# Feed-forward gates and ups with the weights as standing operand, and weight remainders shared with GpSimd

## The chip, the cores and the metric

One core of one Trainium2 chip runs the whole program. The metric is the device time of one execution in microseconds (us), as a median of three runs. Changes of under 0.2% (3.9 us) are not told from none.

## What is computed

The input is 256 tokens of 1024 features. Four layers follow one another (two of a first block, two of a second), and each is feed-forward, mixer, feed-forward:

```python
def swiglu(x, w_gu, w_down):
    g, u = jnp.split(x @ w_gu, 2, axis=-1)
    return (jax.nn.silu(g) * u) @ w_down
...
for l in range(DEPTH):
    f = swiglu(rms_norm(x, ffn1_pre_g[l]), ffn1_w_gu[l], ffn1_w_down[l])
    x = x + 0.5 * rms_norm(f, ffn1_post_g[l])
    m = hybrid_mixer(rms_norm(x, mix_pre_g[l]), ...)
    x = x + rms_norm(m, mix_post_g[l])
    f = swiglu(rms_norm(x, ffn2_pre_g[l]), ffn2_w_gu[l], ffn2_w_down[l])
    x = x + 0.5 * rms_norm(f, ffn2_post_g[l])
```

The second block does the same with other mixers and without the norms behind. The gate and the up matrix are 1024 x 2816 each, the down matrix 2816 x 1024. All is float32. The kernel multiplies in float32r, a rounded form, and so splits each operand in a high part (the rounded value) and a low part (the remainder), and adds three products: high by high, high by low, low by high.

## The kernel before

The tokens lie in two tiles of 128 (t = 0 and 1), and each is a thread of its own (`thread`, a Python generator). Weights come from one packed stream in units of at most 128 x 1024 numbers. For each unit SyncE loads `raw`, then ScalarE or VectorE rounds it to `whi` (`split_hi`), then VectorE subtracts to get the low part `wlo` (`split_lo`). There are 6, 9 and 9 buffers of these; a `whi` and a `wlo` are given back when both threads have used the unit. Hence one thread leads the other by nine units at most.

In a feed-forward block (`ffn`) the tile of activations, transposed, is the standing operand of TensorE and the weights are streamed: for every 128 input features and every 512 columns of gate or up, `mm3` issues three products of 512 columns into `acc`, with `xTh` (high), `xTh` and `xTl` (low) standing:

```python
return [T.matmul(out_, kh, wh, start=start, stop=False), T.matmul(out_, kh, wl, start=False, stop=False),
        T.matmul(out_, kl, wh, start=False, stop=stop)]
```

The result has tokens as rows. ScalarE takes the silu of the gate with the row's norm factor `rs` as a scale (`act`), VectorE multiplies by the up (`fin`), and `t_hilo` transposes the product in pieces of 128 x 128 on TensorE (`tmp<-ident,scr`), since `down` needs the features as rows; its high and low part go to `big0` or `big1`. `down` then runs 22 units with the hidden tile standing, at 12 products of 512 columns a unit for both tiles. Behind it `postnorm` (in the first block) forms the sum of squares on ScalarE, the power -0.5 on GpSimd (`rsyo`), and updates `x` on VectorE; `prenorm` transposes the new `x` and forms `rs`, with another power on GpSimd (`rs`).

The order on each engine is fixed before the run: `Sched` plays the threads through with a cost per instruction (`Engine.make`), takes the most urgent of what can start (a priority from the longest chain behind it, plus a number of the table `BIAS`), and issues in that order; `Either` leaves the choice of engine to it. Where it foresees that TensorE will stand idle, `filler` puts in products with `warm` that compute nothing.

Of the kernel before, what the change touches and what calls it, by code (L numbers as in the profile page):

```python
# [21 lines left out]
P = 128  # L22
# [27 lines left out]
NHI = 9  # L50
NLO = 9
BIAS = {
    ("act", 3): -10.5, ("fin", 3): -1.5, ("fin", 4): -0.5, ("gains", 3): 22.0, ("gains", 4): -12.0,
    ("gate", 3): -7.0, ("gate", 4): -10.5, ("go", 4): -35.5, ("latents", 4): 7.5, ("lru", 4): 3.5, ("norm", 3): 0.5,
    ("norm", 4): 16.4, ("ret_g", 4): -4.5, ("ret_qk", 3): -0.5, ("ret_v", 3): -7.3, ("ret_v", 4): 6.8,
    ("retention", 3): 10.7, ("retention", 4): 1.0, ("sgu", 4): -2.2, ("t_hilo", 4): -5.8, ("thread", 4): -1.6,
    ("xbc", 4): 19.1,
}
IN_ORDER = ("xbc", "xbc2", "zdt", "lru", "sgu", "gate")
OUT_ORDER = (6, 7, 0, 1, 2, 3, 4, 5)  # L60
# [9 lines left out]
X_AFTER = {-1: (0, 0), 0: (1, 0), 2: (0, 1), 4: (1, 1)}  # L70
SCR = 6
LATER = 24
TMP = 4


def _plan():
    units = []

    def proj(specs):
        for cols in specs:  # L80
            n = 2 if units else 1
            for k in range(0, KT, n):
                units.append((list(range(k, k + n)), cols, None))

    def ffn(gate, up, down, l, up0):
        for c0 in range(0, FF, 512):
            if c0 + 512 <= FF:
                proj([[(gate, l, c0, c0 + 512)], [(up, l, up0 + c0, up0 + c0 + 512)]])
            else:
                proj([[(gate, l, c0, FF), (up, l, up0 + c0, up0 + FF)]])  # L90
# [228 lines left out]
class Engine:  # L319
# [233 lines left out]
def program(S, nc, pool, psp, x, wst, pfm, prow, post, lnp, mats, ret_dec, inv, pos, out):  # L553
# [10 lines left out]
    def acc_done(t):  # L564
        S.release(acc_pool[t])
# [38 lines left out]
    def scr_done():  # L604
        S.release(scr_pool)
# [25 lines left out]
    mhalf = pool.tile([P, 3], F32, name="mhalf")  # L631
    nc.vector.memset(mhalf, -0.5)
    early = pool.tile([P, 1], F32, name="early")
# [60 lines left out]
    def split_lo():  # L694
        for i, u in enumerate(units):
# [111 lines left out]
    def t_hilo(src, n, hi, lo, gain=None, evs=None, after=None):  # L807

        for b in range(0, n, 4):
# [20 lines left out]
            if evs is not None and gain is None:  # L830
                S.fire(evs[b // 4])

    def act_t(t):
        h = pool.tile([P, KT, P], F32R, tag=f"xTh{t}", name=f"xTh{t}", align_bytes=256)
        l = pool.tile([P, KT, P], F32R, tag=f"xTl{t}", name=f"xTl{t}", align_bytes=256)
        return h, l

    def prenorm(t, gain, late=False):

# [62 lines left out]
            q.dma_start(pgs[i], post[i:i + 1, :].to_broadcast([P, D]))  # L902
        return pgs[i]

    def ffn(t, gain, pgi, kpi=None):
        kh, kl, evs, rs, rs_ev = prenorm(t, gain, pgi == 0)
        hT = pool.tile([P, 2, FT, P], F32R, tag=f"big{t}", name=f"big{t}", align_bytes=256)
        hh, hl = hT[:, 0], hT[:, 1]
        hev = [Event() for _ in range(6)]

        def act(g, s, n, ev):
            yield rs_ev
            yield A.activation(s[:, :n], g[:, :n], AF.Silu, scale=rs)
# [12 lines left out]
        for c in range(6):
            n = 512 if c < 5 else 256
            g = yield from proj(t, kh, kl, evs)
            s = yield from scr()
            ev = Event()  # L930
            S.spawn(act(g, s, n, ev))
            if c < 5:
                u = yield from proj(t, kh, kl, evs)
            else:
                u = g[:, n:]
            S.spawn(fin(c, s, u[:, :n], n, ev))
            if c == 3 and t == 0:
# [4 lines left out]
        accs = yield from down(t, hh, hl, FT, lambda k: hev[k // 4])  # L942
        if pgi is not None:
            postnorm(t, accs, pgs[pgi], True)
        else:
            addback(t, accs, True)
# [760 lines left out]
    def thread(t):  # L1707
        yield
        for l in range(2):
            yield from ffn(t, fmc("ffn1_pre_g", l) if l else fm0, 3 * l, l)  # L1710
            yield from mixer1(t, l)
            yield from ffn(t, fmc("ffn2_pre_g", l), 3 * l + 2)
        for l in range(2):
            yield from ffn(t, fmc("ffn1_norm_2", l), None)
            yield from mixer2(t, l)
            yield from ffn(t, fmc("ffn2_norm_2", l), None)
        for j in range(2):
            yield xev[t][j]
            sl = slice(j * 512, (j + 1) * 512)
# [82 lines left out]
```

## Time and profile before

| what | value |
|---|---|
| median of 3 runs | 1938.17 us (1938.04 to 1938.38) |
| the profiled execution, time | 1938.33 us |
| the profiled execution, span from first to last instruction | 1936.6 us |
| TensorE matmuls, busy | 1925.4 us, 9247 instructions |
| VectorE, busy | 1494.3 us (77%), 2385 instructions |
| ScalarE, busy | 626.9 us (32%), 1136 instructions |
| GpSimd, busy | 52.9 us (3%), 76 instructions |
| read from HBM | 344 MB, 178 GB/s over the span |

The span leaves out 1.7 us of the execution's time. TensorE's records overlap: one of 512 columns lasts 0.39 us while the next begins 0.23 us after it, so what a product costs is read from start to start. The same holds for VectorE and ScalarE, whose records overlap by some 0.08 and 0.1 us.

### The profile page before, as it was taken

How to read it: one execution, taken by the hardware profiler on the slowest of the kernel's cores; microseconds unless marked ns; L12 is line 12 of the kernel's file. 1: busy time of each engine (PE TensorE's matmuls, PEld its weight loads, DVE VectorE, ACT ScalarE, POOL GpSimd, SP SyncE). 2: the span in 40 equal slices, each digit the busy share in tenths (PEclk: the TensorE clock that was granted, in tenths of full speed). 3: DMA queues.
4: the chain of work that ended last, by engine and by line, in shares of the span. 5: the costliest groups of instructions: out<-in, count | busy, mean ns of one | idle time of the engine just before them, and what ended most of it. 6: DMA issues, size and time to landing. Idle time of an engine off the chain costs nothing.

```text
span 1936.6 us, 24594 instructions
## 1 busy us (share of the span) xinstructions
PE 1925.4 (99%) x9247; PEld 1612.1 (83%) x9247; DVE 1494.3 (77%) x2385; ACT 626.9 (32%) x1136; POOL 52.9 (3%) x76
## 2 busy tenths in 40 slices
PE   9999999999999999999999999999999999999999
PEld 7888988888888898888888888888888888888887
DVE  7977898767767799776777779877777777987774
ACT  5211774211321287320232036631022102662220
POOL 1000010000000001000000000000000000000000
PEclk9999999999999999999999999999999999999999
DMA  8555546555655554654655554356565655545572
GB/s 317 179 191 177 166 148 196 195 167 194 224 177 182 180 168 145 199 190 163 208 186 183 185 180 155 125 178 184 180 203 174 184 181 184 159 126 170 178 217 65
DMA packets 98390, 346.89 MB, mean 179 GB/s; under 512 B 11424, under 2 KB 11680, under 8 KB 98272
## 3 DMA queue, kind: packets, MB, share of 16 engines
q1 hardware_dynamic: 97040, 341.26, 54.3%
q0 software_dynamic: 1088, 4.06, 0.6%
q8 instruction: 72, 1.18, 0.3%
q14 instruction: 46, 0.38, 0.1%
q10 hardware_dynamic: 144, 0.00, 0.0%
HBM read 344.24 MB, written 1.05 MB: 178 GB/s over the span
## 4 chain that ended last, share of the span: by engine, by line
PE 96%; ACT 2%; DVE 1%; POOL 0%; issue 0%; POOLq 0%
PE acc L469 89%; PE tmp L469 7%; ACT big L469 1%; ACT L469 1%; POOL rsyo L469 0%; PE tmp L595 0%; DVE wlo L469 0%; DVE x L469 0%; ACT whi L469 0%; DVE whi L469 0%; DVE big L469 0%; DVE scr L469 0%; ACT scr L469 0%; ACT xTh L469 0%; DVE rswo L469 0%
## 5 line engine op out<-in xcount | busy, mean ns | idle before, releaser
L469 DVE TENSOR_TENSOR wlo<-raw,whi 128x1024 fp32r<-128x1024 f32 (+4 forms) x638 | 765.3, 1201 | 56.1 <-ACT whi L469 43.1
L469 PE MATMUL acc<-whi,xTh 128*128 128x512 f32 (+3 forms) x1888 | 745.1, 395 | 0.0
L469 PE MATMUL acc<-wlo,xTh 128*128 128x512 f32 (+3 forms) x1888 | 729.5, 386 | 1.0 <-DVE wlo L469 1.0
L469 PE MATMUL acc<-whi,xTl 128*128 128x512 f32 (+3 forms) x1888 | 730.0, 387 | 0.0
L469 DVE CAST whi<-raw 128x1024 fp32r<-128x1024 f32 (+1 forms) x402 | 278.4, 692 | 260.7 <-PE acc L469 250.7
L469 PE MATMUL acc<-whi,big 128*128 128x512 f32 x1408 | 457.8, 392 | 0.0
L469 PEld LDWEIGHTS acc<-whi,xTl 128*128 128x128 f32 x1888 | 354.6, 188 | 69.7
L469 PEld LDWEIGHTS acc<-wlo,xTh 128*128 128x128 f32 x1888 | 355.4, 188 | 66.1 <-DVE wlo L469 3.7
L469 PEld LDWEIGHTS acc<-whi,xTh 128*128 128x128 f32 x1888 | 355.0, 188 | 63.8 <-ACT big L469 0.4
L469 ACT CAST whi<-raw 128x1024 fp32r<-128x1024 f32 (+4 forms) x236 | 235.1, 1004 | 303.3 <-PE acc L469 283.7
L469 PEld LDWEIGHTS acc<-whi,big 128*128 128x128 f32 x1408 | 264.5, 188 | 54.0
L469 PE MATMUL acc<-wlo,big 128*128 128x512 f32 x704 | 274.7, 390 | 0.0
L469 ACT ACTIVATE scr<-acc,rs 128x512 f32<-128x512 f32 (+3 forms) x123 | 79.9, 650 | 482.0 <-PE acc L469 477.7
L469 PEld LDWEIGHTS acc<-wlo,big 128*128 128x128 f32 x704 | 132.4, 188 | 26.6 <-DVE wlo L469 0.6
L469 DVE SCALAR_TENSOR_TENSOR scr<-acc,rs,scr 128x512 f32<-128x512 f32 (+1 forms) x96 | 67.3, 705 | 42.0 <-PE acc L469 36.1
L469 ACT CAST big<-tmp 128x512 fp32r<-128x512 f32 (+1 forms) x88 | 47.4, 546 | 158.2 <-PE tmp L469 157.8
L469 PE MATMUL tmp<-ident,scr 128*128 128x128 f32 x484 | 78.4, 273 | 0.1
L469 PEld LDWEIGHTS tmp<-ident,scr 128*128 128x128 f32 x484 | 59.9, 140 | 17.2 <-DVE scr L469 2.9
L469 DVE SCALAR_TENSOR_TENSOR xTl<-tmp,fm,xTh 128x128 fp32r<-128x128 f32 x192 | 58.0, 344 | 13.8 <-ACT xTh L469 12.3
L469 ACT ACTIVATE scr<-acc 128x512 f32<-128x512 f32 x24 | 14.2, 596 | 167.2 <-DVE scr L469 167.2
L469 ACT ACTIVATE xTh<-tmp,fm 128x128 fp32r<-128x128 f32 x167 | 53.3, 365 | 44.9 <-DVE xTl L469 23.7
L469 DVE TENSOR_TENSOR big<-tmp,big 128x512 fp32r<-128x512 f32 (+2 forms) x104 | 64.2, 633 | 3.5 <-ACT big L469 2.8
(222 smaller groups left out, 946.0 us busy)
## 6 DMA issues: line engine op xcount, KB each, us to landing
raw<-in_wst_dram SPq DMA_DIRECT2D x606, 512.0 KB, 3.6
raw<-in_wst_dram SPq DMA_DIRECT2D x28, 384.0 KB, 3.1
raw<-in_wst_dram SPq DMA_DIRECT2D x8, 416.0 KB, 3.1
raw<-in_wst_dram SPq DMA_DIRECT2D x8, 390.0 KB, 3.2
pg<-in_post_dram POOLq DMA_DIRECT2D x5, 512.0 KB, 3.9
raw<-in_wst_dram SPq DMA_DIRECT2D x8, 256.0 KB, 4.7
x<-in_x_dram SPq DMA_DIRECT2D x4, 256.0 KB, 4.9
out_dram<-x SPq DMA_DIRECT2D x4, 256.0 KB, 2.0
```

Source lines behind the costliest of these rows:

```text
L469: op.f(*op.a, **op.k)
```

## The change

The first 512 columns of gate and up of a feed-forward block stay as they were, for each tile by itself. For the other 2304 the roles are swapped (`features`): a unit now is 128 columns of the gate (or of the up) for all 1024 input features, its 128 x 128 pieces stand in TensorE, and the activations of both tiles are streamed. For that the activations lie in one tile `xT`, per 128 features as high of tile 0, high of tile 1, low of tile 0, low of tile 1 (4 x 128 columns). Per piece there are two products: `whi` by all 512 columns, and `wlo` by the first 256. The result has features as rows and the tokens of both tiles as columns, so its transposes fall away. In exchange the two halves of `acc` have to be added (`summed`), and `rs`, which now varies along the columns, has to be spread over all rows once a block (`spread`: a product of ones with a diagonal of `rs`) and multiplied in on VectorE. Both threads wait for each other there (`J["at"]`, `J["end"]`).

Besides, `split_lo` leaves the choice between VectorE and GpSimd to the planner, whose cost for GpSimd becomes 0.1 us plus 1.9 ns an element, and `BIAS` has other numbers.

```diff
 BIAS = {
-    ("act", 3): -10.5, ("fin", 3): -1.5, ("fin", 4): -0.5, ("gains", 3): 22.0, ("gains", 4): -12.0,
+    ("act", 3): -10.5, ("fin", 3): -1.5, ("fin", 4): 0.3, ("gains", 3): -1.9, ("gains", 4): -12.0, ("gate", 3): -1.9,
...
+HEAD = 512
...
-        for c0 in range(0, FF, 512):
...
+        proj([[(gate, l, 0, HEAD)], [(up, l, up0, up0 + HEAD)]])
+        for c0 in range(HEAD, FF, P):
+            units.append((list(range(KT)), [(gate, l, c0, c0 + P)], None))
+            units.append((list(range(KT)), [(up, l, up0 + c0, up0 + c0 + P)], None))
...
-                dur, lat = 0.85, 0.25
+                dur, lat = 0.85 if n < 4 else 0.1 + n * 0.0019, 0.25
...
-                yield V.tensor_tensor(los[i][:, :w], raws[i][:, :w], h, op=ALU.subtract)
+                yield Either(*(e.tensor_tensor(los[i][:, :w], raws[i][:, :w], h, op=ALU.subtract) for e in (V, R)))
...
+    xT = pool.tile([P, KT, 4, P], F32R, name="xT", align_bytes=256)
+
     def act_t(t):
...
+        return xT[:, :, t, :], xT[:, :, 2 + t, :]
...
-        for c in range(6):
-            n = 512 if c < 5 else 256
...
+        S.fire(J["at"][t])
+        if t == 0:
+            yield J["at"][1]
+            yield from features(J, pgi, kpi)
+            S.fire(J["end"])
+        else:
+            yield J["end"]
...
+        def spread():
+            for t in range(2):
+                yield J["rs_ev"][t]
+            d_ = yield from scr()
+            for t in range(2):
+                yield affine(d_[:, t * P:(t + 1) * P], ident, J["rs"][t])
+            p = yield from ps_tmp()
+            yield T.matmul(p[:, :2 * P], ones.to_broadcast([P, P]), d_[:, :2 * P], start=True, stop=True)
...
+        def summed(f, p, v):
+
+            yield copy(v, p[:, 0:2 * P])
+            yield V.tensor_tensor(v, v, p[:, 2 * P:], op=ALU.add)
+            acc_done(f % 2)
+            yield rb_ev
+            yield V.tensor_tensor(v, v, rb, op=ALU.mult)
...
+        def upped(f, p, s, ev):
+            u = s[:, 2 * P:]
+            yield from summed(f, p, u)
+            yield ev
+            yield V.tensor_tensor(u, u, s[:, :2 * P], op=ALU.mult)
+            h = b3(u, 2)
+            yield [copy(hT[:, 0, f, :], h[:, t, :]) for t, hT in enumerate(J["hT"])]
+            yield [V.tensor_tensor(hT[:, 1, f, :], h[:, t, :], hT[:, 0, f, :].bitcast(F32), op=ALU.subtract)
+                   for t, hT in enumerate(J["hT"])]
...
+        for f in range(HEAD // P, FT):
+            b = f % 2
+            ev = Event()
+            for j in range(2):
+                acc = yield from ps_acc(b)
+                hi, lo, _, _ = yield from unit(0)
+                for k in range(KT):
+                    w = slice(k * P, (k + 1) * P)
+                    x4 = xT[:, k].rearrange("p a c -> p (a c)", a=4, c=P)
+                    two = [T.matmul(acc, hi[:, w], x4, start=k == 0, stop=k == KT - 1),
+                           T.matmul(acc[:, 0:2 * P], lo[:, w], x4[:, 0:2 * P], start=False, stop=False)]
+                    yield two if k < KT - 1 else two[::-1]
```

What this does to the order, at three places. In an operand pair of TensorE the streamed one stands first. TensorE in the first feed-forward block, before:

```order
163 L469 MATMUL acc_398<-wlo,xTh_96 128x512
164 L469 MATMUL acc_398<-whi,xTl_97 128x512
165 L469 MATMUL acc_460<-whi,xTh_102 128x512
166 L469 MATMUL acc_460<-wlo,xTh_102 128x512
167 L469 MATMUL acc_460<-whi,xTl_103 128x512
168 L469 MATMUL tmp<-ident,scr 128x128 x3
169 L469 MATMUL acc_398<-whi,xTh_96 128x512
170 L469 MATMUL acc_398<-wlo,xTh_96 128x512
171 L469 MATMUL acc_398<-whi,xTl_97 128x512
```

The same place in the changed kernel, where the joint part begins:

```order
145 L470 MATMUL acc_338<-whi,xT 128x512 x2
146 L470 MATMUL acc_338<-wlo,xT 128x512
147 L470 MATMUL acc_338<-whi,xT 128x512
148 L470 MATMUL tmp<-ident,scr 128x128
149 L470 MATMUL acc_423<-xT,whi 128x512
150 L470 MATMUL acc_423<-xT,wlo 128x256
151 L470 MATMUL acc_423<-xT,whi 128x512
152 L470 MATMUL acc_423<-xT,wlo 128x256
```

What was three products of 512 columns per tile, broken by transposes, became pairs of 512 and 256 columns for both tiles. In the whole program 3456 products of 512 columns go, 2304 pairs come, and 288 of the transposes `tmp<-ident,scr` go (484 before, 196 now).

VectorE in the middle of the joint part of the second feed-forward block (layer 0), one feature block (a gate and an up unit):

```order
675 L470 CAST whi<-raw 128x1024
676 L470 TENSOR_TENSOR scr<-scr,acc_4283 128x256
677 L470 TENSOR_TENSOR wlo<-raw,whi 128x1024
678 L470 TENSOR_TENSOR big_3197<-scr,big_3197 128x128
679 L470 TENSOR_TENSOR big_3268<-scr,big_3268 128x128
680 L470 TENSOR_TENSOR scr<-scr 128x256
681 L470 CAST whi<-raw 128x1024
682 L470 TENSOR_TENSOR scr<-scr,acc_4313 128x256
683 L470 TENSOR_TENSOR wlo<-raw,whi 128x1024
684 L470 TENSOR_TENSOR scr<-scr,rb 128x256 x2
```

Such a round stands there instead of casts and subtractions with a multiplication and a subtraction of 512 columns per tile between. All 36 subtractions `wlo` of each joint part stayed on VectorE, and 34 or 35 of the 36 casts `whi` are there too.

GpSimd between the first mixer and the next feed-forward block, before:

```order
25 L469 TENSOR_TENSOR rsyb_0_2748<-rswb_0_2746,mhalf 128x1
26 L469 TENSOR_TENSOR rsyb_1_2876<-rswb_1_2874,mhalf 128x1
27 L469 TENSOR_TENSOR rsyo_0_2895<-rswo_0_2893,mhalf 128x1
28 L469 TENSOR_TENSOR rs_0_2870<-rsw_0_2972,mhalf 128x1
29 L469 TENSOR_TENSOR rsyo_1_3045<-rswo_1_3043,mhalf 128x1
30 L469 TENSOR_TENSOR rs_1_3010<-rsw_1_3097,mhalf 128x1
```

The same place in the changed kernel:

```order
37 L470 TENSOR_TENSOR wlo<-raw,whi 128x1024
38 L470 TENSOR_TENSOR rsyb_0_3019<-rswb_0_3017,small 128x1
39 L470 TENSOR_TENSOR wlo<-raw,whi 128x1024
40 L470 TENSOR_TENSOR rsyb_1_3130<-rswb_1_3128,small 128x1
41 L470 TENSOR_TENSOR rsyo_0_3217<-rswo_0_3215,small 128x1
42 L470 TENSOR_TENSOR wlo<-raw,whi 128x1024
43 L470 TENSOR_TENSOR rs_0_3195<-rsw_0_3285,small 128x1
44 L470 TENSOR_TENSOR rsyo_1_3320<-rswo_1_3318,small 128x1
45 L470 TENSOR_TENSOR rs_1_3266<-rsw_1_3379,small 128x1
46 L470 TENSOR_TENSOR wlo<-raw,whi 128x1024
```

Subtractions of weight units now stand in one queue with the powers that the norms need; 72 of them went to GpSimd in the whole program, all outside of the joint parts. In the changed kernel TensorE has 94 filler products, where there were 59 (loads of `warm` counted): 17 of them stand in each of the first block's two passages from the second feed-forward block to what comes next, 20 between the first mixer and its feed-forward block, and none at the end of the second mixer, where 16 stood.

## Rows read from the trace of the kernel before

**Rows 1.** The page, parts 1 and 2: busy time by engine; granted clock by slice.

```profile
PE 1925.4 (99%) x9247; PEld 1612.1 (83%) x9247; DVE 1494.3 (77%) x2385; ACT 626.9 (32%) x1136; POOL 52.9 (3%) x76
...
PEclk9999999999999999999999999999999999999999
```

**Rows 2.** The page, part 4: the chain that ended last, by engine.

```profile
PE 96%; ACT 2%; DVE 1%; POOL 0%; issue 0%; POOLq 0%
```

**Rows 3.** Chain in order of time, a down projection: start us, us, engine, count.

```profile
143.00 44.91 PE acc L469 x198
```

**Rows 4.** TensorE timeline, 257 to 261 us: start us, us, engine, line, operation.

```profile
257.20 0.34 PE L469 MATMUL acc<-whi,xTl 128*128 128x384 f32 x1
...
260.35 0.34 PE L469 MATMUL acc<-whi,xTl 128*128 128x384 f32 x1
```

**Rows 5.** TensorE timeline, 303 to 305 us: transposes between two products.

```profile
303.63 0.39 PE L469 MATMUL acc<-whi,xTl 128*128 128x512 f32 x1
303.86 0.60 PE L469 MATMUL tmp<-ident,x 128*128 128x128 f32 x4
304.21 0.48 PE L469 MATMUL acc<-whi,xTh 128*128 128x512 f32 x1
304.53 0.40 PE L469 MATMUL acc<-wlo,xTh 128*128 128x512 f32 x1
```

**Rows 6.** TensorE weight loads, timeline at 239.7 us.

```profile
239.70 0.19 PEld L469 LDWEIGHTS acc<-whi,xTh 128*128 128x128 f32 x1
239.81 0.19 PEld L469 LDWEIGHTS acc<-wlo,xTh 128*128 128x128 f32 x1
```

**Rows 7.** VectorE timeline, 470 to 481 us, end of the second feed-forward block.

```profile
472.71 0.69 DVE L469 CAST whi<-raw 128x1024 fp32r<-128x1024 f32 x1 [0.77 <-PE acc L469]
473.32 0.68 DVE L469 TENSOR_TENSOR scr<-acc,pg 128x512 f32<-128x512 f32 x1
...
478.62 0.42 DVE L469 TENSOR_TENSOR big<-tmp,big 128x256 fp32r<-128x256 f32 x1
478.95 0.74 DVE L469 SCALAR_TENSOR_TENSOR x<-scr,rsyo,x 128x512 f32<-128x512 f32 x1
479.61 1.22 DVE L469 TENSOR_TENSOR wlo<-raw,whi 128x1024 fp32r<-128x1024 f32 x1
480.75 0.60 DVE L469 SCALAR_TENSOR_TENSOR xTl<-tmp,fm,xTh 128x128 fp32r<-128x128 f32 x2
```

**Rows 8.** Windows: sum over the eight gate-and-up stages (950 us): busy by engine.

```profile
sum 950.00, PE 949.92 PEld 783.02 DVE 713.44 ACT 221.69 POOL 18.51; mean PE 118.74 PEld 97.88 DVE 89.18 ACT 27.71 POOL 2.31
```

**Rows 9.** Windows: sum over the four mixers (439 us): busy by engine.

```profile
sum 439.00, PE 435.19 PEld 384.40 DVE 396.42 ACT 305.03 POOL 20.63; mean PE 108.80 PEld 96.10 DVE 99.10 ACT 76.26 POOL 5.16
```

**Rows 10.** TensorE timeline, end of the first mixer; idle before in brackets.

```profile
267.63 0.66 PE L469 MATMUL tmp<-ident,big 128*128 128x128 f32 x4 [0.64 <-DVE big L469]
...
271.64 0.55 PE L469 MATMUL tmp<-ident,big 128*128 128x128 f32 x3 [1.04 <-ACT big L469]
```

**Rows 11.** Chain in order of time, first mixer: the filler products.

```profile
272.19 1.20 PE tmp L595 x11
```

**Rows 12.** TensorE timeline, second feed-forward block to the next layer's first.

```profile
478.76 0.66 PE L469 MATMUL tmp<-ident,x 128*128 128x128 f32 x4 [0.38 <-DVE x L469]
```

**Rows 13.** GpSimd timeline, 25 to 30 us.

```profile
25.13 4.34 POOL L469 TENSOR_TENSOR rs<-rsw,mhalf 128x1 f32<-128x1 f32 x1 [7.55 <-DVE rsw L469]
```

**Rows 14.** VectorE timeline, the same stretch.

```profile
24.97 2.35 DVE L469 TENSOR_TENSOR wlo<-raw,whi 128x1024 fp32r<-128x1024 f32 x2
27.24 0.68 DVE L469 CAST whi<-raw 128x1024 fp32r<-128x1024 f32 x1
...
29.06 0.75 DVE L469 SCALAR_TENSOR_TENSOR scr<-acc,rs,scr 128x512 f32<-128x512 f32 x1
```

**Rows 15.** Groups of instructions, GpSimd: count | busy us, mean ns | idle before.

```profile
L469 POOL TENSOR_TENSOR rsyo<-rswo,mhalf 128x1 f32<-128x1 f32 x12 | 11.5, 962 | 612.0 <-DVE rswo L469 612.0
...
L469 POOL TENSOR_TENSOR rsyb<-rswb,mhalf 128x1 f32<-128x1 f32 x4 | 2.2, 548 | 54.0 <-DVE rswb L469 54.0
```

More of the change, by code (lines that the diff above doesn't have):

```diff
@@ L52 @@
 BIAS = {
-    ("act", 3): -10.5, ("fin", 3): -1.5, ("fin", 4): -0.5, ("gains", 3): 22.0, ("gains", 4): -12.0,
[L54 to L57, printed above, removed]
+    ("act", 3): -10.5, ("fin", 3): -1.5, ("fin", 4): 0.3, ("gains", 3): -1.9, ("gains", 4): -12.0, ("gate", 3): -1.9,
+    ("gate", 4): -10.5, ("go", 3): -0.6, ("go", 4): -35.5, ("heads", 4): 17.0, ("latents", 3): 17.5,
+    ("latents", 4): 6.8, ("lru", 4): 3.5, ("norm", 3): -1.9, ("norm", 4): 16.4, ("prologue", 5): 0.1,
+    ("ret_g", 4): -4.5, ("ret_qk", 3): 2.2, ("ret_v", 3): -7.3, ("ret_v", 4): 2.4, ("retention", 4): 1.0,
+    ("sgu", 4): -2.2, ("split_lo", 2): -3.8, ("spread", 3): -3.6, ("t_hilo", 4): -5.8, ("tell", 4): -0.1,
+    ("thread", 4): -4.1, ("xbc", 4): 19.1,
 }
@@ L85, in ffn @@
     def ffn(gate, up, down, l, up0):
-        for c0 in range(0, FF, 512):
[L87 to L90, printed above, removed]
+        proj([[(gate, l, 0, HEAD)], [(up, l, up0, up0 + HEAD)]])
+        for c0 in range(HEAD, FF, P):
+            units.append((list(range(KT)), [(gate, l, c0, c0 + P)], None))
+            units.append((list(range(KT)), [(up, l, up0 + c0, up0 + c0 + P)], None))
         for k in range(FT):
@@ L630, in program @@
     nc.vector.memset(warm, 0.5)
-    mhalf = pool.tile([P, 3], F32, name="mhalf")
+    small = pool.tile([P, 8], F32, name="small")
+    mhalf, ones, early = small[:, 0:3], small[:, 3:4], small[:, 4:5]
     nc.vector.memset(mhalf, -0.5)
-    early = pool.tile([P, 1], F32, name="early")
+    nc.vector.memset(ones, 1.0)
     nc.scalar.activation(early, mhalf[:, 0:1], AF.Silu)
@@ L831, in t_hilo @@
                 S.fire(evs[b // 4])
+    xT = pool.tile([P, KT, 4, P], F32R, name="xT", align_bytes=256)
     def act_t(t):
-        h = pool.tile([P, KT, P], F32R, tag=f"xTh{t}", name=f"xTh{t}", align_bytes=256)
-        l = pool.tile([P, KT, P], F32R, tag=f"xTl{t}", name=f"xTl{t}", align_bytes=256)
-        return h, l
+        return xT[:, :, t, :], xT[:, :, 2 + t, :]
     def prenorm(t, gain, late=False):
@@ L903, in post_gain, with ffn @@
         return pgs[i]
-    def ffn(t, gain, pgi, kpi=None):
+    joint = {}
+    def ffn(t, n_, gain, pgi, kpi=None):
         kh, kl, evs, rs, rs_ev = prenorm(t, gain, pgi == 0)
-        hT = pool.tile([P, 2, FT, P], F32R, tag=f"big{t}", name=f"big{t}", align_bytes=256)
+        J = joint.setdefault(n_, dict(rs=[None, None], hT=[None, None], rs_ev=[Event(), Event()], at=[Event(), Event()], end=Event(),
+                                      hev=[Event() for _ in range(FT)]))
+        hev = J["hev"]
+        hT = J["hT"][t] = pool.tile([P, 2, FT, P], F32R, tag=f"big{t}", name=f"big{t}", align_bytes=256)
@@ L908, in ffn, with tell, act @@
         hh, hl = hT[:, 0], hT[:, 1]
-        hev = [Event() for _ in range(6)]
-        def act(g, s, n, ev):
+        def tell():
             yield rs_ev
-            yield A.activation(s[:, :n], g[:, :n], AF.Silu, scale=rs)
-            if n == 512:
-                acc_done(t)
+            J["rs"][t] = rs
+            S.fire(J["rs_ev"][t])
+        S.spawn(tell())
+        def act(g, s, ev):
+            yield rs_ev
+            yield A.activation(s, g, AF.Silu, scale=rs)
+            acc_done(t)
@@ L916, in act, with fin @@
             S.fire(ev)
-        def fin(c, s, u, n, ev):
+        def fin(s, u, ev):
             yield ev
-            yield V.scalar_tensor_tensor(s[:, :n], u, rs, s[:, :n], op0=ALU.mult, op1=ALU.mult)
+            yield V.scalar_tensor_tensor(s, u, rs, s, op0=ALU.mult, op1=ALU.mult)
             acc_done(t)
             yield
-            yield from t_hilo(s, n // P, hh[:, 4 * c:4 * c + n // P], hl[:, 4 * c:4 * c + n // P], None, [hev[c]])
+            yield from t_hilo(s, 4, hh[:, 0:4], hl[:, 0:4], None, [head_ev])
@@ L924, in fin @@
             scr_done()
-        for c in range(6):
-            n = 512 if c < 5 else 256
-            g = yield from proj(t, kh, kl, evs)
-            s = yield from scr()
-            ev = Event()
[L931 to L937, printed above, removed]
+        head_ev = Event()
+        g = yield from proj(t, kh, kl, evs)
@@ new lines, in ffn @@
+        s = yield from scr()
+        ev = Event()
+        S.spawn(act(g, s, ev))
+        u = yield from proj(t, kh, kl, evs)
+        S.spawn(fin(s, u, ev))
+        S.fire(J["at"][t])
[5 more added lines that the diff above has]
+            yield J["end"]
+        accs = yield from down(t, hh, hl, FT, lambda k: head_ev if k < HEAD // P else hev[k])
+        if pgi is not None:
+            postnorm(t, accs, pgs[pgi], True)
+        else:
+            addback(t, accs, True)
@@ new lines, in features, with gated @@
+    def features(J, pgi, kpi):
+        rb = pool.tile([P, 2 * P], F32, tag="rb", name="rb")
+        rb_ev = Event()
+        def spread():
[6 more added lines that the diff above has]
+            yield T.matmul(p[:, :2 * P], ones.to_broadcast([P, P]), d_[:, :2 * P], start=True, stop=True)
+            scr_done()
+            yield copy(rb, p[:, :2 * P])
+            tmp_done()
+            S.fire(rb_ev)
+        S.spawn(spread())
+        def summed(f, p, v):
[4 more added lines that the diff above has]
+            yield V.tensor_tensor(v, v, rb, op=ALU.mult)
+        def gated(f, p, s, ev):
+            g = s[:, :2 * P]
+            yield from summed(f, p, g)
+            yield A.activation(g, g, AF.Silu)
+            S.fire(ev)
+        def upped(f, p, s, ev):
[7 more added lines that the diff above has]
+                   for t, hT in enumerate(J["hT"])]
+            scr_done()
+            S.fire(J["hev"][f])
+        for f in range(HEAD // P, FT):
+            b = f % 2
+            ev = Event()
+            for j in range(2):
[7 more added lines that the diff above has]
+                    yield two if k < KT - 1 else two[::-1]
+                cursor[1] += 1
+                unit_done(0)
+                unit_done(1)
+                if not j:
+                    s = yield from scr()
+                S.spawn((upped if j else gated)(f, acc, s, ev))
+                yield
+            if f == 12:
@@ L941, in ffn @@
                     keep(kpi)
[L942 to L946, printed above, removed]
     K = {}
@@ L1709, in thread @@
         for l in range(2):
-            yield from ffn(t, fmc("ffn1_pre_g", l) if l else fm0, 3 * l, l)
+            yield from ffn(t, (0, l), fmc("ffn1_pre_g", l) if l else fm0, 3 * l, l)
             yield from mixer1(t, l)
-            yield from ffn(t, fmc("ffn2_pre_g", l), 3 * l + 2)
+            yield from ffn(t, (1, l), fmc("ffn2_pre_g", l), 3 * l + 2)
         for l in range(2):
-            yield from ffn(t, fmc("ffn1_norm_2", l), None)
+            yield from ffn(t, (2, l), fmc("ffn1_norm_2", l), None)
             yield from mixer2(t, l)
-            yield from ffn(t, fmc("ffn2_norm_2", l), None)
+            yield from ffn(t, (3, l), fmc("ffn2_norm_2", l), None)
         for j in range(2):
```

## The prediction

> **What bounds the kernel now.** I read the page first, then the chain of waits, then single stretches. [...] VectorE is the next engine. In the eight gate-and-up stages it is busy for 713 of 950 us [rows 8], in the four mixers for 396 of 439 us [rows 9].
>
> TensorE's records overlap, so I count from start to start. [...] Four transposes stand between products at 303.86 us; from the start of the product ahead of them to the start of the second one behind them it is 0.90 us [rows 5]. Less two products that leaves 0.446, or 0.1116 for a transpose, its share of the change-over included. TensorE has little idle time to give back; its long waits lie at the ends of the first block's mixers, 0.64 and 1.04 us [rows 10], filled up beyond that with filler products.
>
> **The change part by part.** All sums are against the profiled execution, 1938.33 us (span 1936.6 and 1.7 around it); the median of the runs is 0.16 lower, which I neglect.
>
> *Products.* 3456 products of 512 columns go: 783.8 us. 2304 pairs of 512 and 256 columns come. No product of 256 float32r columns stands in this trace. [...] It costs no more than one of 384, 0.175 [rows 4]. At the other end two weight loads begin no closer than 0.11 us [rows 6], and each product needs one, so 0.110 is the least. I take 0.121, since it is a line through two neighbours. The pairs then take 2304 x 0.3478 = 801.3 us: **+17.5 us** (-7.8 at 0.110, +142 at 0.175). [...]
>
> [...]
>
> *Transposes.* 288 go, at 0.1116: **-32.1 us**. They were on TensorE's path, with nothing beside them that they hid under.
>
> *Spreading the norm factor.* Eight products in plain float32 by 256 columns. The nearest row is the transpose, 0.11 for 128 columns: 0.22 each, **+1.8 us** (0.9 if the width costs nothing, 3.6 if it costs double).
>
> *Fillers.* 35 more, at 1.20 us for eleven [rows 11]: **+3.8 us**. They stand where one tile has to wait for its norm and the other has nothing left to cover it: the second feed-forward block now lets tile 0 lead by three units only. They take the place of idle time, and are counted as such.
>
> TensorE's own work thus falls by 9.0 us. Now the waits.
>
> *Waits before the fillers.* In mid-run the order has ten places with fillers, where it had four. A filler comes in only behind a wait. At such passages the trace has 0.38 [rows 12], 0.64 and 1.04 us [rows 10]. I take 0.4 for the six additional ones, **+2.4 us** (0 to 6.2), and **-0.9 us** because two of the four were in the second mixer, where they held 1.7 and not 0.8, and are gone.
>
> *VectorE in the joint part.* Per feature block of 128 it has two casts, two subtractions of 1024 columns, five operations of 256 columns and two of 128. From start to start these take 0.61, 1.14 (479.61 to 480.75) and 0.33 us [rows 7], and 0.20 for 128 columns on the line between the last two. Together 5.55 us. TensorE's two units take 16 x 0.348 = 5.57 us. VectorE goes from three quarters busy to full. I still put this at **0 us**: the nine weight buffers let it be some units ahead, and a pair of accumulators is wanted again only one feature block, 5.6 us, later, so a delay has to exceed that before TensorE feels it. If the cover is gone, the rival below prices it. ScalarE has the copies, the silu and two casts of 128 columns; it was busy for 222 of 950 us [rows 8] and hides them.
>
> *GpSimd.* 72 subtractions leave VectorE, all outside of the joint parts, and queue with the powers of the norms. GpSimd was idle for nearly all of the run, so its time itself costs nothing. But a power of one column, which takes 0.55 us where it is least disturbed [rows 15], took 4.34 [rows 13] while VectorE ran subtractions and a cast back to back, and ended only when VectorE came to an operation that reads PSUM [rows 14]. So the two engines do not run beside each other there, and a piece of 1024 columns will meet this far more often. What stands behind it on GpSimd is `rsyo` or `rsyb`, whose mean is 0.96 and 0.55 [rows 15]. The difference, 0.4, is what such a meeting costs now. I charge it at the four passages where TensorE has nothing else (second feed-forward block to the next, and mixer to feed-forward, in both layers of the first block): **+1.6 us**. The bounds are -1.7 (VectorE is rid of 72 pieces, and the waits of one mixer's end vanish) and +18 (the third rival).
>
> [...] The rows show GpSimd blocked; that VectorE is blocked by a long GpSimd instruction no row here shows. [...]
>
> Sum: +17.5 - 32.1 + 1.8 + 3.8 + 2.4 - 0.9 + 1.6 = -5.9, so 1938.3 - 5.9 = **1932.4 us**.
>
> **The rivals.**
>
> *The new meetings eat the gain.* Each of the eight feed-forward blocks now has two points at which both tiles must have arrived, the entry of the joint part and its end. For it: the order puts tile 0's first transposes at the very end of some joint parts, just ahead of `down`. Against it: the order shows no fillers at the entries. With the 0.38 us of rows 12 at all 16 points it is 6.1 us: 1938.5, no difference.
>
> *VectorE becomes the bound of the joint part.* For it: 5.55 of 5.57 us. Against: the buffers, and the times above are from start to start already. It decides when a round takes over 5.57 + 5.6/18 = 5.88 us. At 10% more than 5.55, 6.1 us, it falls 18 x 0.53 = 9.5 us behind in a block, of which 5.6 are covered: 8 x 3.9 = 31 us, 1964.
>
> *GpSimd's queue delays the norms.* Sixteen powers (twelve `rsyo`, four `rsyb`) sit in chains that TensorE waits for. For it: the 4.34 us of rows 13 and VectorE's 90% in the mixers. Against: the other tile's work covers most of these chains. If each is late by one piece at no better than VectorE's own 1.14 us, it is 18.2 us instead of the 1.6 in the sum: 1949, slower. It decides at a mean of 0.7 us ((5.9 + 1.6 + 3.9)/16), from which on the kernel is slower.
>
> *The narrow product does not hide the next weight load.* The records of loads last 0.19 us [rows 6]. If a product had to wait for the end of the record, 256 columns would cost 0.19 and the sum would be 159 us higher: 2091. Against it: products of 384 columns follow each other every 0.175, and the loads start 0.11 apart.
>
> That the change does not do what it says is out: the order has the pairs and the missing transposes.
>
> **How the numbers follow.** A measurement of this kernel tells 0.2%, 3.9 us, from no change: under 1934.3 is faster, over 1942.1 slower. My forecast lies 2 us inside of faster. Work removed from a bound engine is the surest part of it, so I give the forecast's case, faster, 0.54; the meetings 0.24, the same; the GpSimd queue 0.11, VectorE 0.07 and the weight load 0.04, all slower, 0.22. The range runs from 1918 (no waits added at all, -3.1, and the narrow product halfway to its lower bound, 0.1155, -12.7, give 1917) to 1951 (the GpSimd rival, and a little of VectorE's). It leaves out most of VectorE's rival, the weight load and the ends of the other cases, some 0.18.
>
> **What would show it.** From start to start, a pair of 512 and 256 columns in the joint part takes 0.348 us, 16 of them 5.57 us, without gaps. There are 196 transposes `tmp<-ident,scr`. VectorE is nearly full in the joint parts and TensorE's waits for `wlo` or for accumulators stay under 1 us per block. Subtractions on GpSimd, of a length that this trace does not hold, lie beside a VectorE that waits. The prediction is wrong in its reason if the pair takes over 0.36 us, if TensorE waits in the joint parts, or if the passages between blocks cost over 10 us more than now.

## The result, and the profile after

The changed kernel takes **2021.24 us** (median; 2021.07 to 2021.64) against 1938.11 (1937.91 to 1938.38): ratio 1.0429, 95% interval 1.0413 to 1.0444. It is slower by 83 us where 1932.4 was forecast, far outside the range. The profiled execution has a span of 2019.4 us.

The page of the changed kernel, parts 1, 2 and 4, answers to [rows 1, 2]:

```profile
PE 1949.8 (97%) x10162; PEld 1657.7 (82%) x10162; DVE 1764.2 (87%) x3282; ACT 671.4 (33%) x1610; POOL 226.2 (11%) x148
...
PE   9999889999999989999999998999999999899999
...
POOL 3001332000300132100020002110000000211000
PEclk9999999999999989999999998999999999999999
...
PE 82%; DVE 15%; issue 2%; ACT 1%; POOL 0%; DMA 0%; SPq 0%; DVEq 0%; ACTq 0%; POOLq 0%
```

TensorE stood idle for 11 us of the span before (1936.6 - 1925.4); it is 70 us now (2019.4 - 1949.8). VectorE's share of the chain went from 1% to 15%. The five slices of 50 us in which TensorE is less busy lie in the four mixers, where GpSimd is at work, and two of them show a lower clock, too. The joint parts are not the place. Their windows, summed over all eight [rows 8], and then the chain within the second one:

```profile
sum 820.20, PE 820.20 PEld 713.90 DVE 793.52 ACT 219.42 POOL 16.05; mean PE 102.53 PEld 89.24 DVE 99.19 ACT 27.43 POOL 2.01
```

```profile
366.06 81.08 PE acc L470 x460
```

TensorE is busy from end to end there, with VectorE at 97% (793.5 of 820.2 us). The chain's 460 products are 230 pairs, 0.3525 us each.

The mixers are the place. GpSimd's and then VectorE's timeline in the second one (start us, us; idle before in brackets):

```profile
738.26 9.93 POOL L470 TENSOR_TENSOR wlo<-raw,whi 128x1024 fp32r<-128x1024 f32 x4 [11.59 <-ACT whi L470]
753.55 1.81 POOL L470 TENSOR_TENSOR wlo<-raw,whi 128x768 fp32r<-128x768 f32 x1 [5.36 <-ACT whi L470]
```

```profile
739.26 9.87 DVE L470 SCALAR_TENSOR_TENSOR big<-big,fm 128x128 f32<-128x128 f32 x7
...
749.12 1.91 DVE L470 SCALAR_TENSOR_TENSOR big<-big,fm 128x128 f32<-128x128 f32 x7
...
753.60 1.78 DVE L470 TENSOR_TENSOR ad<-spr,na 128x6 f32<-128x6 f32 x1
755.30 0.15 DVE L470 SCALAR_TENSOR_TENSOR spe<-dt 128x6 f32<-128x6 f32 x1
```

Seven VectorE instructions of 128 columns take 9.87 us while GpSimd runs four pieces (a **piece** is one of the 72 subtractions there), and the next seven of the same kind, with GpSimd idle, 1.91. At 753.60 an instruction of six columns takes 1.78 us, and ends (755.38) with the piece that began 50 ns ahead of it (755.36).

What TensorE does meanwhile: its timeline, the waits from 740 to 756 us (total, times, longest), and windows with the granted clock, the third number from the right:

```profile
744.79 0.40 PE L470 MATMUL acc<-whi,xT 128*128 128x512 f32 x1
752.07 0.90 PE L470 MATMUL tmp<-ident,big 128*128 128x128 f32 x3 [6.88 <-ACT big L470]
752.63 0.78 PE L470 MATMUL acc<-whi,xT 128*128 128x512 f32 x1
```

```profile
ACT big L470 <- DVE big L470: 7.9, 1, 7.9
...
PE tmp L470 <- ACT big L470: 6.9, 1, 6.9
```

```profile
740.00:745.00 5.00, 5.00 (x27) 4.44 (x25) 5.00 (x3) 3.16 (x7) 5.00 (x3) 1.00 0.28 79
745.00:752.00 7.00, 0.19 (x1) 0.00 (x0) 7.00 (x19) 0.93 (x2) 3.19 (x2) 0.77 0.73 224
752.00:755.00 3.00, 2.93 (x10) 2.45 (x10) 3.00 (x9) 2.98 (x5) 1.45 (x1) 0.50 0.01 4
755.00:758.00 3.00, 2.58 (x19) 2.51 (x19) 2.71 (x9) 1.43 (x7) 0.36 (x1) 0.91 0.17 45
```

TensorE waits for ScalarE, which waits for VectorE, which GpSimd holds up: 6.9 us. Behind the wait the granted clock is 0.50 (752 to 755 us), and the first product's record is twice as long (0.78 against 0.40). So this wait costs more than its own length.

It also goes the other way round, earlier in the same mixer. From 720.73 us sixteen of VectorE's instructions of 128 columns run at their usual pace, and a piece that begins among them lasts 4.64 us, where the mean of its width is 2.25:

```profile
720.73 4.28 DVE L470 SCALAR_TENSOR_TENSOR big<-big,fm 128x128 f32<-128x128 f32 x16
```

```profile
722.04 4.64 POOL L470 TENSOR_TENSOR wlo<-raw,whi 128x768 fp32r<-128x768 f32 x1 [1.91 <-ACT whi L470]
```

The same groups of VectorE's work, before and after (count | busy us, mean ns | idle before):

```profile
L469 DVE CAST whi<-raw 128x1024 fp32r<-128x1024 f32 x400 | 277.4, 693 | 256.6 <-PE acc L469 250.7 <-DMA raw<-in_wst_dram 2.4
...
L469 DVE SCALAR_TENSOR_TENSOR xTl<-tmp,fm,xTh 128x128 fp32r<-128x128 f32 x192 | 58.0, 344 | 13.8 <-ACT xTh L469 12.3 <-PE acc L469 1.1
...
L469 DVE SCALAR_TENSOR_TENSOR big<-big,fm 128x128 f32<-128x128 f32 x84 | 23.1, 344 | 0.0
...
L469 DVE SCALAR_TENSOR_TENSOR x<-scr,rsyo,x 128x512 f32<-128x512 f32 x24 | 17.8, 747 | 6.5 <-POOL rsyo L469 6.5
```

```profile
L470 DVE CAST whi<-raw 128x1024 fp32r<-128x1024 f32 x487 | 357.1, 733 | 139.1 <-PE acc L470 128.5 <-issue 7.6 <-DMA raw<-in_wst_dram 1.1
...
L470 DVE SCALAR_TENSOR_TENSOR xT<-tmp,fm,xT 128x128 fp32r<-128x128 f32 x192 | 57.8, 342 | 12.9 <-ACT xT L470 10.3 <-PE acc L470 1.9
...
L470 DVE SCALAR_TENSOR_TENSOR big<-big,fm 128x128 f32<-128x128 f32 x84 | 43.4, 589 | 0.0
...
L470 DVE SCALAR_TENSOR_TENSOR x<-scr,rsyo,x 128x512 f32<-128x512 f32 x24 | 30.1, 1262 | 3.3 <-POOL rsyo L470 3.3
```

The first, third and fourth group, which read and write SBUF alone, became longer on average (0.73, 0.59, 1.26 us); `xT<-tmp,fm,xT` (before, `xTl<-tmp,fm,xTh`), which reads PSUM and SBUF, did not, though 37 of its 192 lie beside a piece. If each VectorE record that overlaps a GpSimd instruction is set against the median of its own kind elsewhere in the trace, the excess is 109 us; before it is 0.3 us. I call this the **stretch** below. Pieces on GpSimd have a mean of 2.57 us for 1024 columns, and a median over all widths of 2.40.

My theory was then: a piece shuts VectorE out, its chains in the mixers are late, and TensorE waits. The rival: the new stages, or the mixers' order under the new table of numbers, cost the time by themselves.

### The profile page after: what moved, and what is told of

The parts are those of the page before. It is cut to its first block, busy times and chain, and to the rows that moved or that the text cites. A ratio compares the mean times of both kernels' runs of the same rounds, so it can differ in the third digit from the quotient of the medians.

```text
span 2019.4 us, 27979 instructions
## 1 busy us (share of the span) xinstructions
PE 1949.8 (97%) x10162; PEld 1657.7 (82%) x10162; DVE 1764.2 (87%) x3282; ACT 671.4 (33%) x1610; POOL 226.2 (11%) x148
## 3 DMA queue, kind: packets, MB, share of 16 engines
HBM read 344.24 MB, written 1.05 MB: 171 GB/s over the span
## 4 chain that ended last, share of the span: by engine, by line
PE 82%; DVE 15%; issue 2%; ACT 1%; POOL 0%; DMA 0%; SPq 0%; DVEq 0%; ACTq 0%; POOLq 0%
PE acc L470 78%; DVE big L470 5%; PE tmp L470 3%; DVE scr L470 2%; DVE wlo L470 2%; DVE whi L470 1%; DVE x L470 1%; DVE xT L470 1%; DVE mx L470 0%; DVE rsqh L470 0%; ACT scr L470 0%; DVE spp L470 0%; DVE rsyr L470 0%; DMA x<-in_x_dram 0%; POOL wlo L470 0%
## 5 line engine op out<-in xcount | busy, mean ns | idle before, releaser
L470 PE MATMUL acc<-xT,whi 128*128 128x512 f32 x2304 | 795.4, 398 | 0.0
L470 DVE TENSOR_TENSOR wlo<-raw,whi 128x1024 fp32r<-128x1024 f32 (+2 forms) x566 | 681.7, 1206 | 16.9 <-ACT whi L470 11.3
L470 PE MATMUL acc<-xT,wlo 128*128 128x256 f32 x2304 | 599.7, 281 | 0.0
L470 PE MATMUL acc<-whi,xT 128*128 128x512 f32 (+3 forms) x1472 | 484.2, 393 | 10.9 <-DVE xT L470 9.6
L470 PEld LDWEIGHTS acc<-xT,whi 128*128 128x128 f32 x2304 | 414.6, 188 | 79.7
L470 PEld LDWEIGHTS acc<-xT,wlo 128*128 128x128 f32 x2304 | 435.0, 189 | 26.3
L470 PEld LDWEIGHTS acc<-whi,xT 128*128 128x128 f32 x1472 | 279.8, 191 | 61.0 <-DVE xT L470 15.4
L470 PE MATMUL acc<-wlo,xT 128*128 128x512 f32 (+3 forms) x736 | 283.9, 386 | 3.2 <-POOL wlo L470 2.5
L470 POOL TENSOR_TENSOR wlo<-raw,whi 128x1024 fp32r<-128x1024 f32 (+3 forms) x72 | 174.5, 2432 | 491.1 <-ACT whi L470 349.1
L470 PEld LDWEIGHTS acc<-wlo,xT 128*128 128x128 f32 x736 | 141.2, 192 | 25.4 <-POOL wlo L470 3.0
```

The source lines that it names most:

```text
L470: op.f(*op.a, **op.k)
```

## The experiments

**All low parts on VectorE**, the rest of the change kept, the order planned anew:

```
-  yield Either(*(e.tensor_tensor(los[i]..., op=ALU.subtract) for e in (V, R)))
+  yield V.tensor_tensor(los[i]..., op=ALU.subtract)
```

> The changed kernel with all 658 low parts on VectorE (none on GpSimd), the order planned anew; everything else of the change is in it. Theory 1 (a GpSimd piece and VectorE shut each other out: the VectorE records beside the 72 pieces are about 110 us longer in sum than the same records without a piece beside them, and TensorE waits for VectorE's chains in the mixers): the stretching is gone, the time falls to 1935 to 1950 us; TensorE's idle time in the mixers comes down from about 90 us to under 30. Theory 2 (the stages of the joint features, or the mixers' order that was planned with the new table of numbers, cost the time by themselves): 1990 us or more, with VectorE's records short and the waits still there.

Measured 1944.75 us (1943.48 to 1944.95), ratio to before 1.0032 (1.0019 to 1.0045). Theory 1. The stretch is 1 us. The page's first line shows TensorE idle for 13 us (1942.9 - 1930.0):

```profile
PE 1930.0 (99%) x10218; PEld 1649.3 (85%) x10218; DVE 1713.2 (88%) x3326; ACT 685.7 (35%) x1635; POOL 52.7 (3%) x76
```

Of these 13 us, 5 lie in the mixers (from the end of `down` to the next joint part). The changed kernel has 59 there, not the 90 that my expectation started from. What the time also says: in this order the rest of the change brings nothing, it loses 6.5 us.

**The same order, the 72 pieces issued on VectorE:**

```
+  ops = [e.tensor_tensor(los[i]..., op=ALU.subtract) for e in (V, R)]
+  ops[1].f = nc.vector.tensor_tensor
+  yield Either(*ops)
```

> The changed kernel with its order untouched: the 72 pieces that were planned for GpSimd are issued at the same places on VectorE instead, which takes on some 75 us of work that it was not planned to have. Theory 1 (the two engines shut each other out): VectorE loses about 110 us of stretching for 75 us of work, so the time falls by 60 to 85 us, to 1935 to 1960 us. Theory 2 (order or joint stages): 2010 to 2040 us, since the order is the same and VectorE has more to do.

Measured 1983.63 us (1981.86 to 1985.42), 1.0234 (1.0219 to 1.0250). The time falls, as theory 1 has it and theory 2 has not, but by 38 us and not 60 to 85. The stretch is gone (0.4 us), yet TensorE still idles for 30 us in the mixers. I had taken the stretch lost and the work added as if both cost TensorE alike; my reading, which no run tests, is that this order leaves VectorE no room there for the subtractions. Even so the 72 cost less on VectorE than on GpSimd.

**The kernel before, with this part of the change alone** (the two GpSimd lines of the diff, the order planned anew; 61 pieces):

> The kernel before with this one part of the change alone: the low parts may go to GpSimd by the same cost, and 61 of 658 do (72 in the change). No joint features, no new table. Theory 1 (shutting out): about 61 x 1.5 us of VectorE's time is lost, some 61 x 1.1 us of it seen at the end: 1990 to 2015 us, VectorE's records beside the pieces longer by some 90 us in sum. Theory 2 (joint stages or the table): 1930 to 1942 us, as before, since nothing of the joint stages is in it.

Measured 2002.15 us (2001.55 to 2004.42), 1.0333 (1.0316 to 1.0350): 64 us lost without any of the joint stages, 1.05 per piece, as theory 1 said. The stretch is 76 us. The chain by engine, and then two groups, show the picture of the change:

```profile
PE 81%; DVE 11%; issue 5%; ACT 1%; DMA 1%; POOL 0%; SPq 0%; DVEq 0%; ACTq 0%; POOLq 0%
```

```profile
L469 POOL TENSOR_TENSOR wlo<-raw,whi 128x1024 fp32r<-128x1024 f32 x36 | 90.7, 2524 | 404.9 <-DVE whi L469 291.3 <-ACT whi L469 84.8 <-issue 21.4
...
L469 DVE SCALAR_TENSOR_TENSOR big<-big,fm 128x128 f32<-128x128 f32 x84 | 42.3, 574 | 0.0
```

That leaves the question what of a piece does it. Three kernels keep the change's order and alter only what GpSimd executes at the 72 places.

**Zeros written, nothing read:**

```
+  ops[1].f = lambda o, a, b, op: nc.gpsimd.memset(o.bitcast(F32), 0.0)
```

> The changed kernel, same order, but each of the 72 GpSimd pieces only writes zeros into its tile and reads nothing (this leaves out the subtraction of 72 of 658 low parts). Theory 1 in its narrow form (VectorE is shut out by a GpSimd instruction that reads SBUF): VectorE's records beside the pieces are not lengthened, and the time falls below the first kernel with all on VectorE (1945), to 1930 to 1942 us, which is also what the order would have given had the pieces been free. In its wide form (any long GpSimd instruction in SBUF, writing too): every piece still shuts VectorE out for as long as it lasts; with pieces of 1.0 to 2.4 us, 1965 to 2021 us.

Measured 1936.60 us (1936.33 to 1937.36), 0.9992 (0.9982 to 1.0002). The narrow form. The page, parts 1 and 4:

```profile
PE 1926.4 (100%) x10162; PEld 1646.5 (85%) x10162; DVE 1667.2 (86%) x3282; ACT 669.8 (35%) x1610; POOL 116.0 (6%) x148
...
PE 95%; DVE 2%; ACT 2%; issue 0%; DMA 0%; SPq 0%; POOL 0%; DVEq 0%; ACTq 0%
```

The windows of the four mixers, each from the end of `down` to the start of the next joint part, so that both kernels have the same work in them (the next block's first 512 columns included): the second one and the sum, of this kernel and then of the changed one (the granted clock is the third number from the right of a window's row):

```profile
674.60:794.10 119.50, 118.69 (x653) 104.32 (x652) 107.63 (x288) 87.89 (x161) 20.97 (x25) 1.00 0.51 169
...
sum 500.40, PE 497.42 PEld 430.03 DVE 428.64 ACT 316.38 POOL 73.05; mean PE 124.36 PEld 107.51 DVE 107.16 ACT 79.09 POOL 18.26
```

```profile
702.80:844.50 141.70, 125.44 (x653) 108.98 (x652) 128.15 (x288) 87.96 (x161) 43.66 (x25) 0.94 0.44 143
...
sum 578.90, PE 519.99 PEld 442.72 DVE 504.74 ACT 317.08 POOL 151.97; mean PE 130.00 PEld 110.68 DVE 126.18 ACT 79.27 POOL 37.99
```

Groups of this kernel:

```profile
L705 POOL MEMSET wlo<- 128x1024 f32 x53 | 51.2, 968 | 419.5 <-PE acc L470 419.2
...
L470 DVE CAST whi<-raw 128x1024 fp32r<-128x1024 f32 x487 | 343.8, 706 | 144.5 <-PE acc L470 139.9 <-DMA raw<-in_wst_dram 1.7
L470 DVE SCALAR_TENSOR_TENSOR big<-big,fm 128x128 f32<-128x128 f32 x84 | 22.6, 345 | 0.0
```

The instructions of TensorE, VectorE and ScalarE and their order are the same. The mixers take 578.9 us with the pieces and 500.4 with the zeros. VectorE is busy there for 76 us longer with the same instructions (504.7 against 428.6), and TensorE idles for 58.9 us instead of 3.0. So the pieces cost 2021.2 - 1936.6 = **84.6 us**, 1.2 each, and 78.5 of them lie in the mixers. By the pages, 61.2 of them are idle time of TensorE (69.6 less 8.4), and 23.4 are longer busy time (1949.8 less 1926.4), with a mean granted clock of 0.989 instead of 1.000. Two things differ beside the reading: a memset takes 0.97 us and not 2.4, and it does not wait for `raw` and `whi`. That a low part from GpSimd comes late is not what TensorE waits for in the changed kernel. Its waits for one come to 2.5 us in all:

```profile
PE acc L470 <- POOL wlo L470: 2.5, 1, 2.5
```

The stretch beside the zeros is 10 us, and 6.6 of it lie in the casts (0.706 us on average, against 0.693 in the kernel before).

**A copy of the raw weights:**

```
+  ops[1].f = lambda o, a, b, op: nc.gpsimd.tensor_copy(o, a)
```

> The same with a copy of the raw weights in place of the subtraction: GpSimd reads one SBUF tile instead of two and writes one (this, too, leaves out the subtraction of these 72 low parts). If one reading input is enough to shut VectorE out, VectorE still loses the remainder of each piece, about 1.5 us x 72 scaled by the piece's length against 2.4 us: 1975 to 2021 us. If it takes two inputs: 1930 to 1945 us, records of VectorE unchanged.

Measured 1954.66 us (1952.72 to 1956.58), 1.0085 (1.0070 to 1.0100). Between the two forecasts.

```profile
L705 POOL CAST wlo<-raw 128x1024 fp32r<-128x1024 f32 x53 | 64.6, 1222 | 413.6 <-PE acc L470 374.9 <-issue 32.7 <-DMA raw<-in_wst_dram 5.8
...
L470 DVE SCALAR_TENSOR_TENSOR big<-big,fm 128x128 f32<-128x128 f32 x84 | 29.4, 420 | 0.0
```

Now a copy's typical record is as long as the memset's (median 1.05 against 0.95 us), yet the stretch is 35 us and not 10, and 18 us are lost. One reading input was enough to lengthen VectorE's records (`big<-big,fm` 0.420 us on average, against 0.345 beside the zeros), two were not needed. The price does not follow the length alone: scaled by it (1.05 of 2.40 us) the 84.6 us would be 37 and the time 1974. Why it is 18 stays open. A copy also waits for `raw`, which a memset does not, and no run parts that from the reading.

**Each piece as two halves:**

```
+  n = size(o) // 2
+  for q in (slice(0, n), slice(n, 2 * n)):
+      nc.gpsimd.tensor_tensor(o[:, q], a[:, q], b[:, q], op=op)
```

> The changed kernel, same order, each GpSimd piece as two instructions of half the columns, one behind the other. If VectorE is shut out until the GpSimd instruction that runs has ended (records show a VectorE instruction that starts within a piece ending 0.14 us behind it), it now waits for half a piece at most: its lengthening falls from 110 us to 50 to 75 us, the time to 1965 to 2000 us, and GpSimd's halves wait for VectorE instead. If the two engines only share a rate (each slowed while the other runs), the sum stays: 2010 to 2030 us.

Measured 2005.48 us (2003.53 to 2007.48), 1.0348 (1.0332 to 1.0363): a miss, between the two forecasts. The stretch is 90 us, not 50 to 75.

```profile
L699 POOL TENSOR_TENSOR wlo<-raw,whi 128x512 fp32r<-128x512 f32 x106 | 155.2, 1488 | 430.9 <-ACT whi L470 313.7 <-DVE whi L470 79.1 <-issue 36.7
...
L470 DVE SCALAR_TENSOR_TENSOR big<-big,fm 128x128 f32<-128x128 f32 x84 | 44.1, 597 | 0.0
```

In the second mixer, beside eight halves in a row, VectorE's timeline has

```profile
736.51 7.55 DVE L470 SCALAR_TENSOR_TENSOR big<-big,fm 128x128 f32<-128x128 f32 x6
```

which is 1.26 us for one, about one per half; beside the whole pieces it was 1.41 (9.87 for seven). VectorE is held up less per meeting and more often, so for this group nothing is gained (0.597 us on average, against 0.589 with whole pieces). Of the 84.6 us cutting the pieces up brings back 16.

**The 52 pieces within the mixers as zeros, the 20 outside real:**

```
+  nth[0] += 1
+  if nth[0] - 1 in MIXERS:
+      nc.gpsimd.memset(o.bitcast(F32), 0.0)
+  else:
+      nc.gpsimd.tensor_tensor(o, a, b, op=op)
```

> The changed kernel, same order; the 52 pieces that run in the four mixers only write zeros (this leaves out the subtraction of those low parts), the 20 outside them (the first stage, the feed-forward stages and their ends) are the change's own. If a piece costs time only where TensorE waits for VectorE's chains, that is in the mixers: at most 8 us over the kernel with all 72 written as zeros (1936.6), so 1936 to 1944 us, though VectorE's records beside these 20 are lengthened by some 1 us each. If every piece costs the same 84.6 / 72 = 1.2 us wherever it stands: 1936.6 + 23 = 1960 us.

Measured 1941.57 us (1940.89 to 1942.90), 1.0018 (1.0008 to 1.0028): 5.0 us over the kernel with 72 zeros, 0.25 per piece, though the stretch rose by 17 us (to 28). By difference the 52 pieces in the mixers carry 79.6 us, 1.5 each, which agrees with the 78.5 us of the windows above. Two of the other 20 run at 31.18 and 35.91 us in the changed kernel, within the first joint part, so not all 72 lie outside of the joint parts. The same meeting cost little (0.25 us a piece) where TensorE had products that wait for nobody.

**Products of one width behind each other** (with all low parts on VectorE; per unit one product of 512 columns, eight of 256, seven of 512, where the change alternates):

```
...
+  seq = his_[:1] + los_ + his_[1:]
   for k in range(KT):
...
-      yield two if k < KT - 1 else two[::-1]
+      yield seq[2 * k:2 * k + 2]
```

> The first of these kernels with one more edit: in the 288 units of the joint features the 8 products of 256 columns follow each other behind the first one of 512, then come the other 7 of 512, where the change alternates 512 and 256. Theory A (it is the alternation that makes a pair cost 0.353 us: 0.236 from the start of a 512-column product to the next start, 0.118 from a 256-column one, against 0.227 and 0.115 within a row of one width): a pair falls to about 0.342, 2304 x 0.011 = 25 us less than the first of these kernels. Theory B (the cost belongs to the 256-column product and its weight load): within 4 us of the first.

Measured 1937.33 us (1936.34 to 1938.05), 0.9996 (0.9986 to 1.0005): 7.4 us less than alternating, between the two theories: a third of what A forecast, and more than B's 4. The chain in the second joint part, alternating (the first of these kernels) and then grouped:

```profile
344.96 73.28 PE acc L470 x416
```

```profile
343.04 72.99 PE acc L470 x418
```

The pair costs 73.28/208 = 0.3523 and 72.99/209 = 0.3492 us, and 2304 x 0.0031 = 7.1 us is the gain that was measured. In TensorE's timeline of the grouped kernel

```profile
399.94 2.00 PE L470 MATMUL acc<-xT,whi 128*128 128x512 f32 x8
401.78 1.11 PE L470 MATMUL acc<-xT,wlo 128*128 128x256 f32 x8
402.73 2.00 PE L470 MATMUL acc<-xT,whi 128*128 128x512 f32 x8
```

eight products of 512 take 1.84 us from start to start, 0.230 each, and eight of 256 take 0.95, 0.119 each: not the 0.227 and 0.115 that theory A had. This version beats the changed kernel by 84 us and is level with the one before. Of the versions that compute everything it is the fastest; none beats the kernel before by what can be measured.

## Why the prediction was wrong, point by point

*The step that failed* is "GpSimd ... its time itself costs nothing ... I charge it at the four passages ...: +1.6 us", with bounds of -1.7 and +18. By the kernel with zeros it is +84.6. I had read the 4.34 us power of [rows 13, 14] as GpSimd being held up by VectorE, and asked only what stands behind it on GpSimd's queue. The same exclusion the other way round, VectorE held up by a piece of 2.4 us, was left out of the sum and of every rival, because no row of the trace showed it: GpSimd ran nothing long before. But VectorE's 90% in the mixers [rows 9] were in my hand, and I did not ask what a piece might cost VectorE there. The third rival named the right engine and the right sign, and the wrong victim. Of the sixteen powers that it counts, the mean of the twelve `rsyo` fell from 0.96 to 0.69 us, and that of the four `rsyb` rose from 0.55 to 1.01: 12.3 us in all, where it was 13.7 [rows 15]. Nor did they queue for long: none started more than 0.5 us after its input was ready.

```profile
L470 POOL TENSOR_TENSOR rsyo<-rswo,small 128x1 f32<-128x1 f32 x12 | 8.3, 689 | 585.9 <-DVE rswo L470 585.9
...
L470 POOL TENSOR_TENSOR rsyb<-rswb,small 128x1 f32<-128x1 f32 x4 | 4.0, 1006 | 23.7 <-DVE rswb L470 23.7
```

The changed kernel's trace shows this other side, with 109 us of stretch, and 84.6 us of time go with it; a piece of 1024 columns took 2.57 us on average. Beside memsets `big<-big,fm` has 0.345 us, as before, and the cast 0.706 us instead of 0.693. I should have made a VectorE held up by the pieces a rival with a price, 72 pieces by the length of a piece (174.5 us in all in the changed kernel), and a range that covered it would have reached over 2021.

*Products* (+17.5): mis-sized. Alternating they take 2304 x 0.3525 = 812 us, +28; grouped, 0.3492, +21. The 783.8 us, and the 0.1116 of a transpose, count a product of 512 columns at 44.91/198 = 0.2268 us [rows 3]; one of 384 has 0.175, eighteen in 3.15 us [rows 4]. No run shows the 0.121 that the sum takes for 256 columns. The line through these two widths gives 0.123, as an estimate, and the grouped kernel showed 0.119, with 0.230 for 512. So the pair of the forecast (0.3478) was 1.4 ns too low when each width runs in a row, and alternating adds 3.3 ns. The 0.11 of [rows 6] is the distance of one pair of weight loads and no limit: in the trace before, 40 loads for products into `tmp` begin 0.05 to 0.09 us behind the one ahead.

*Transposes* (-32.1), *fillers* (+3.8) and *VectorE in the joint part* (0): 196 transposes `tmp<-ident,scr` are left of 484. From the start of each to the next start on TensorE they took 44.4 us before and 19.5 in the kernel with 72 zeros, 24.9 less; what the change-over back to products adds is not in that, so the 32.1 are not shown in full. The fillers, read in the same way, went from 8.1 to 11.8 us, +3.7, as forecast. Of VectorE's 97% in the joint parts TensorE felt nothing (820.2 us busy of 820.2); with that and 0.3525 us a pair the rival on it and the one on the weight load fall.

*The waits and meetings* came to nothing that stands out: with 72 zeros TensorE idles for 8.4 us in all, where it was 11.2 before the change. That kernel takes 1936.6 us, where the sum without its GpSimd term says 1930.8; the products explain that and more (+10.9). The other terms together came out 5.1 us lower than summed, and no run divides that among them.

*The planner's part.* With the pieces back on VectorE it needs 10218 instructions on TensorE instead of 10162: 56 more fillers, 6 us at [rows 11] and 7.0 from start to start in the trace, of the 8.2 us between 1944.75 and what the zeros gave, 1936.6. A filler stands where TensorE would wait, so this tells where the time goes, not why the order needs it.

Not settled: why the halves lose 69 us when the longest wait is halved was only argued, from one group of instructions. No run has a long piece that reads nothing, so how much of the 84.6 us is the reading and how much the length of a piece that reads is not parted either.

## What to carry to other kernels

Before work is moved to an idle engine, ask which of the busy ones becomes slower beside it, and price the meeting on both: here 2.4 us on GpSimd cost VectorE 1.5 us of stretch, more than the 1.2 us that the same subtraction takes on VectorE. Here it mattered most where TensorE waits for VectorE's chains, so count the pieces by stage: 52 in the mixers cost 1.5 us each, 20 elsewhere 0.25. And a planner that prices an operation by its own duration alone, as this one does, can choose such a trade by itself.

## What the runs showed of the hardware

- A VectorE instruction of six columns that started within a GpSimd subtraction took 1.78 us, where the next one of six columns took 0.15, and ended 0.02 us behind the piece. The changed kernel has eight such records of four or six columns, of 1.5 to 2.3 us, and each ends 0.02 to 0.03 us behind its piece.
- It was not always VectorE that waited: sixteen instructions of 128 columns kept their pace (4.28 us), and the piece beside them lasted 4.64 us instead of some 2.25.
- A GpSimd memset (0.97 us) hardly touched VectorE, a GpSimd copy (median 1.05 us) did: stretch of 10 and 35 us over 72 of them.
- VectorE instructions with a PSUM input went on beside the pieces unchanged (`xT<-tmp,fm,xT` 0.342 against 0.344 us). The 76 records beside pieces that read or write `tmp` or `acc`, which lie in PSUM, have a stretch of 0.0 us in sum; the 139 others have 108.
- After a 6.9 us wait of TensorE the granted clock was 0.50 for the next 3 us, and the first product's record there 0.78 us instead of 0.40.
- Widths that alternate cost more here: 0.3525 us for a pair of 512 and 256 columns, 0.3492 when each width runs in a row.
